# A hybrid decoder step: the sample group's HGRN update moved from the projection into the attention's filler work, and the page table read by one load

## The chip, the cores and the metric

One core of one Trainium2 chip. The metric is the device time of one execution in microseconds (us). A kernel's time is the median of several executions; the profile describes one execution.

## The reference, cut to what matters

One layer for two groups of tokens with the same weights: a prompt of 1024 tokens and a sample group of 8 sequences with one new token each and 1024 tokens of past. The layer is a projection (1024 to 3864 columns), a sparse attention with three branches (compressed, selected and window blocks; the sample group's past lies in paged caches), an HGRN2 recurrence with 4 heads of 128 x 128 state, an output projection and a gated embedding term.

The part that the change moves is the sample group's recurrence step. With one token per sequence it is, for every sequence b and head h,

```python
S_new = exp(log f)[..., None] * S + k[..., None] * v[None, :]
o = q @ S_new
```

where `S` (`state_hgrn`, 8 sequences x 4 heads x 128 x 128 fp32, 2 MB) is read, `S_new` is an output, and `o` is normalised and goes into the output projection. The page table (8 sequences x 8 pages, int32) gives for each sequence the rows of the caches: with 16 rows of a page on 16 partitions, partition p of column b needs `16 * page_table[b, p // 16] + p % 16`.

## The kernel before, in words

All matmuls work on fp32 numbers taken apart into a high and a low part: `split` (L50, L51) writes `hi` by a copy and `lo` by a subtraction, and `mm` (L42) is called with the combinations, so that most matmuls and casts carry the lines L42, L50 and L51. `load_w` (L222) loads weights in eight 128-row pieces (`w_raw`, L233, 3 buffers) and makes `w_hi` on ACT (L238) and `w_lo` on DVE (L239).

The program has these stages. Input tokens are loaded, normalised and transposed. The projection (`project`, L281) makes groups of columns: `tok` with tokens on partitions, `feat` with features on partitions. Between them stands the prompt group's recurrence: `hgrn_a` (L469) builds, per head, the masked products `AT` (with tiles `QK`, `PR`, `PQ` and predicated copies at L490, L513, L520 and L540), and `hgrn_b` (L566) makes states and outputs `O` (scaled at L608 on POOL, transposed at L612 on PE). The compressed keys follow, then the attention (`attention`, L618): 16 units of (128 queries, key group), cut into blocks. After every second block `attention` takes one step from the generator `side_work` (L640), which before holds the sample group's attention (`sample_attention`, L1000: gathers of cached rows into `sg`, stores of their second half to `VS`, window loads into `sg`, transposes, scores, softmax), and then the first steps of the last stage. The last stage is the output projection.

Each engine executes its instructions in a fixed order. That order is made when the kernel is built: a scheduler runs over all instructions with a cost model and priorities (the attention's blocks and the filler steps have their own), and it keeps the dependences and whatever `after` (L44) adds as an ordering without a semaphore. A DMA is issued from the queue of an engine; nearly all loads here are issued by SP, which also follows its order: an issue that has to wait for a buffer holds back the issues behind it.

The sample group's recurrence before is `hgrn_sample` (L422), a generator that `project` steps by hand, mostly around the last of the prompt's heads. For each head it loads the whole batch's state into a 128 x 1024 tile (L437, tag `S`) and the values, broadcast over the partitions, into another (`vb`, L439, tag `O`), from `v_d`, a copy of `vs` in DRAM. DVE multiplies `vb` by k (L441), POOL the state by f (L442), DVE adds (L443), SP stores the new state (L444), ACT and DVE split it into `S0h` and `S0l` (tag `F`), and PE makes 16 small matmuls per head with `qp`, a zeroed tile (L433) in which the 8 columns of q stand so that the results of all sequences and heads add up in one PSUM tile. Tags `S`, `O` and `F` are the ones that the prompt's recurrence uses: they share its buffers.

`page_index` (L645) reads the page table with 8 loads (L651) of 16 x 8 elements, each repeating a page number over 16 partitions, and makes `pidx` on DVE (L658). `project` calls it after the first recurrence heads; the scheduler may put its loads earlier.

Of the kernel before, what the change touches and what calls it, by code (L numbers as in the profile page):

```python
# [7 lines left out]
F32 = mybir.dt.float32  # L8
# [12 lines left out]
NB = 8  # L21
# [6 lines left out]
class Kernel:  # L28
# [195 lines left out]
    def load_w(self, src, *parts):  # L224

        nc = self.nc
        out = []
        width = sum(p[1] for p in parts)
        for k in range(8):
            raw = self.wpool.tile([128, 512], F32, name="w_raw", bufs=3)[:, :width]  # L230
            o = 0
            for c0, n in parts:
                dma = nc.sync.dma_start(raw[:, o:o + n], src[k * 128:(k + 1) * 128, c0:c0 + n])  # L233
# [13 lines left out]
        return out  # L247
# [32 lines left out]
    def project(self, ctx):  # L280
# [62 lines left out]
        go = lambda n: [next(smp, None) for _ in range(n)]  # L343
        for h in range(2, 4):
            st = self.hgrn_a(h, Q[h], K[h], F[h])
            go(2 if h == 3 else 0)
            self.hgrn_b(h, *st)
            go(1 if h == 3 else 0)

        def ev_z(dst, scale):  # L350
            def ev(f, ts, p):
# [38 lines left out]
        for _ in smp:  # L390
            pass
        self.aux_rows(hp)
        self.tok(C_KC, 256, ev_kv(0))
        self.tok(C_KS, 256, ev_kv(1))
# [24 lines left out]
                nc.sync.dma_start(self.V[:, br, :, h, :64], self.kv_d[1 + br].rearrange("(i p) c -> p i c", p=128)[:, :, 128 + 64 * h:192 + 64 * h])  # L419
        self.feat((C_ZB, 4, ev_z(self.zb_d, self.hgn)), ps=1)  # L420

    def hgrn_sample(self):  # L422

        nc, hp, a = self.nc, self.hp, self.a
        f, k, q = (self.sfkq[:, i] for i in range(3))
        v_d = self.dram.tile([NB, 512], F32, name="v_d")
        self.after(self.pidma, nc.sync.dma_start(v_d, self.vs))
        o = hp.tile([32, 128], F32, name="so", bufs=1)
        for h in range(4):
            yield  # L430
            po = self.ps_t.tile([128, 512], F32, name="pt")[:64, :128]
            qp = hp.tile([128, NB, 64], F32R, name="qp", bufs=1)
            nc.vector.tensor_scalar(qp.rearrange("p (a c) d -> p a (c d)", c=2), self.ones[:, None, :].to_broadcast([128, 4, 128]), 0.0, None, op0=OP.mult)  # L433
            qv = qp.rearrange("p b c -> p (b c)")
            self.split(qv[:, h * NB:h * NB + 456:65], qv[:, 32 + h * NB:32 + h * NB + 456:65], q[:, h], nc.vector, nc.vector)
            S = hp.tile([128, NB, 128], F32, name="S0", tag="S")
            nc.sync.dma_start(S, a["state_hgrn"][0, :, h].rearrange("b k v -> k b v"))  # L437
            vb = hp.tile([128, NB, 128], F32, name="vb", tag="O")
            nc.sync.dma_start(vb, bass.AP(tensor=v_d.tensor, offset=v_d.offset + h * 128, ap=[[0, 128], [512, NB], [1, 128]]))  # L439
            bc = lambda t: t[:, h, :, None].to_broadcast([128, NB, 128])  # L440
            nc.vector.tensor_tensor(vb, vb, bc(k), op=OP.mult)  # L441
            nc.gpsimd.tensor_tensor(S, S, bc(f), op=OP.mult)  # L442
            nc.vector.tensor_tensor(S, S, vb, op=OP.add)  # L443
            nc.sync.dma_start(a["hgrn_state_sample"][0, :, h].rearrange("b k v -> k b v"), S)  # L444
            hi = hp.tile([128, NB, 128], F32R, name="S0h", tag="F")
            lo = hp.tile([128, NB, 128], F32R, name="S0l", tag="F")
            self.split(hi, lo, S, nc.scalar, nc.vector)
            for b in range(NB):
                self.mm(po, qp[:, b], hi[:, b], b == 0, False)
                self.mm(po[:32], qp[:, b, :32], lo[:, b], False, b == NB - 1)  # L450
            if h:
# [4 lines left out]
        sq = hp.tile([32, 128], F32, name="ssq", bufs=1)  # L456
        ss = hp.tile([128, 1], F32, name="sr", bufs=1)[:32]
        nc.scalar.activation(sq, o, AF.Square, accum_out=ss)
        nc.vector.tensor_scalar(ss, ss, 1.0 / 128, EPS, op0=OP.mult, op1=OP.add)
        r = hp.tile([128, 1], F32, name="srs", bufs=1)[:32]  # L460
        self.rsqrt(hp, r, ss)
        nc.vector.tensor_scalar(o, o, r, None, op0=OP.mult)
        pt = self.ps_t.tile([128, 512], F32, name="pt")[:, :32]
        nc.tensor.transpose(pt, o, self.ident[:32, :32])
        oT = hp.tile([128, 32], F32, name="soT", bufs=1)
# [173 lines left out]

    def side_work(self):  # L640
        with ExitStack() as c:
            yield from self.sample_attention(c)
        yield from self.finish_setup(self.fctx)

    def page_index(self, pool):  # L645

        nc = self.nc
        pt = self.a["page_table"]
        raw = pool.tile([128, NB], I32, name="pt_raw", bufs=1)
        for i in range(8):  # L650
            dma = nc.sync.dma_start(raw[16 * i:16 * i + 16], bass.AP(tensor=pt.tensor, offset=pt.offset + i, ap=[[0, 16], [8, NB]]))  # L651
            if i == 0:
                self.pidma = dma
        lane = pool.tile([128, NB], I32, name="pt_lane", bufs=1)
        nc.gpsimd.iota(lane, pattern=[[0, NB]], base=0, channel_multiplier=1)
        nc.vector.tensor_scalar(lane, lane, 15, None, op0=OP.bitwise_and)
        self.pidx = self.cp.tile([128, NB], I32, name="pidx")
        nc.vector.scalar_tensor_tensor(self.pidx, raw, 16.0, lane, op0=OP.mult, op1=OP.add)  # L658
# [280 lines left out]
    def branches(self, qb, g, i):  # L939
# [455 lines left out]
```

## Time and profile before

| | |
|---|---|
| time, median of 3 runs | 1086.51 us (1083.82 to 1089.3) |
| time of the profiled execution | 1086.7 us |
| its span in the trace | 1085.0 us |
| mean granted TensorE clock | 0.991 of full speed |
| PE busy | 1047.7 us (97%) |
| DVE busy | 617.8 us (57%) |
| ACT busy | 388.4 us (36%) |
| POOL busy | 243.9 us (22%) |
| moved by DMA | 116.44 MB, mean 107 GB/s |

How to read the rows: times are in us from the start of the span. A row of the timeline has start, length, engine, line, operation, output tile <- input tiles, and in brackets how long the engine had been idle before it and what ended the wait. A row of the chain of waits has start, length and the work that the end of the program hung on at that time. A row of the windows has, for a stretch, the busy time of each engine with the number of instructions, the granted TensorE clock, the share of the 16 DMA engines and GB/s. Matmuls are pipelined: the length of one is longer than the distance to the next.

### The profile page before, as it was taken

The page shows a single profiled execution, that of the slowest core. Times are in us where ns is not written, and L with a number is a line of the kernel's source. Part 1 is how long each engine was busy: PE and PEld are TensorE (multiplying, and loading weights), DVE is VectorE, ACT ScalarE, POOL GpSimd, SP SyncE. Part 2 cuts the span into 40 slices and gives each one's busy share as a digit, 9 for nine tenths or more (in the row PEclk, how much of TensorE's full clock was granted, in tenths as well). Part 3 has the DMA queues.
Part 4 walks back from the last instruction along what each step waited for, and adds up shares of the span by engine and source line. Part 5 has one row for each costly group of instructions (what it writes and reads, how often), then busy time and mean ns, then how long its engine had stood idle before and what let it go on. Part 6 is the DMA issues. An engine that isn't in the chain of part 4 may idle for free.

```text
span 1085.0 us, 18918 instructions
## 1 busy us (share of the span) xinstructions
PE 1047.7 (97%) x7021; PEld 933.6 (86%) x7021; DVE 617.8 (57%) x1822; ACT 388.4 (36%) x786; POOL 243.9 (22%) x276
## 2 busy tenths in 40 slices
PE   4999999999899999999989999999999999999998
PEld 3898799999889899999968888888788888778876
DVE  6847565665494634543665656766665686471223
ACT  4622234313132335432234544553554232241112
POOL 0014232331041133002032211121323133131111
PEclk9999999999989999999989999999999999999999
DMA  6212023323464766403568611001831573121110
GB/s 195 79 29 69 11 72 100 117 89 119 131 176 142 214 210 211 148 1 107 129 215 266 154 29 51 20 21 53 227 106 40 161 209 90 41 97 49 49 35 30
DMA packets 118815, 116.44 MB, mean 107 GB/s; under 512 B 18710, under 2 KB 100974, under 8 KB 116420
## 3 DMA queue, kind: packets, MB, share of 16 engines
q1 hardware_dynamic: 97220, 79.46, 25.7%
q10 hardware_dynamic: 19200, 19.01, 5.1%
q0 software_dynamic: 2304, 16.78, 4.5%
q8 instruction: 55, 0.90, 0.4%
q14 instruction: 36, 0.29, 0.1%
HBM read 84.84 MB, written 29.31 MB: 105 GB/s over the span
## 4 chain that ended last, share of the span: by engine, by line
PE 82%; DMA 9%; DVE 4%; issue 2%; ACT 2%; POOL 1%; SPq 0%; ACTq 0%; DVEq 0%; POOLq 0%
PE pa L42 39%; PE pb L42 26%; PE ph L42 9%; PE pt L42 4%; DMA vb<-v_d 2%; DMA w_raw<-w_in 2%; PE ph L717 1%; PE pa L1125 1%; DMA fw_raw<-w_out 1%; DMA fw_raw<-ple_gate 1%; DMA x_in<-x_prompt 1%; DVE fw_lo L51 1%; PE ph L1319 1%; DMA gpre<-g_pre 0%; DMA f_oa<-oa_d 0%
## 5 line engine op out<-in xcount | busy, mean ns | idle before, releaser
L42 PEld LDWEIGHTS pb<-V,P 128*128 128x128 f32 x1056 | 141.8, 191 | 12.1 <-POOL P L960 1.2
L42 PE MATMUL pb<-V,P 128*128 128x128 f32 x1056 | 148.1, 276 | 0.4 <-DVE mx L909 0.4
L42 PE MATMUL pa<-xhi,w_hi 128*128 128x344 f32 x384 | 126.0, 330 | 2.6 <-ACT w_hi L238 1.1
L42 PE MATMUL pa<-xlo,w_hi 128*128 128x344 f32 x384 | 124.5, 326 | 0.0
L42 PE MATMUL pa<-xhi,w_lo 128*128 128x344 f32 x384 | 123.5, 327 | 0.0
L955 ACT ACTIVATE P<-ph 128x512 f32<-128x512 f32 (+4 forms) x148 | 85.6, 595 | 98.6 <-PE ph L42 69.3
L916 DVE CUSTOM_DVE_ANT_0 junk<-pa,mask 128x320 bf16<-128x320 f32 (+5 forms) x150 | 72.9, 497 | 27.8 <-PE pa L42 26.6
L42 PE MATMUL pa<-w_lo,xhi 128*128 128x256 f32 (+2 forms) x256 | 79.5, 314 | 0.0
L42 PE MATMUL pa<-w_hi,xlo 128*128 128x256 f32 (+2 forms) x256 | 79.2, 314 | 0.0
L42 PE MATMUL pa<-w_hi,xhi 128*128 128x256 f32 (+2 forms) x256 | 78.6, 316 | 0.0
L42 PEld LDWEIGHTS pa<-xhi,w_hi 128*128 128x128 f32 x384 | 73.5, 192 | 4.2 <-ACT w_hi L238 1.7
L238 ACT ACTIVATE w_hi<-w_raw,gpre 128x512 fp32r<-128x512 f32 (+2 forms) x80 | 47.5, 616 | 78.2 <-DMA w_raw<-w_in 43.0
L42 PEld LDWEIGHTS pa<-xlo,w_hi 128*128 128x128 f32 x384 | 73.5, 192 | 0.1
L42 PEld LDWEIGHTS pa<-xhi,w_lo 128*128 128x128 f32 x384 | 73.0, 191 | 0.2
L42 PE MATMUL ph<-QA,KA 128*128 128x512 f32 (+4 forms) x148 | 66.7, 453 | 3.8 <-ACT P L955 2.9
L42 PE MATMUL pa<-KB,QB 65*128 65x320 f32 (+6 forms) x195 | 63.4, 363 | 0.1
L239 DVE SCALAR_TENSOR_TENSOR w_lo<-w_raw,gpre,w_hi 128x512 fp32r<-128x512 f32 (+2 forms) x80 | 50.6, 653 | 21.4 <-ACT w_hi L238 20.7
L42 PE MATMUL pa<-fw_hi,yh 128*128 128x512 f32 (+1 forms) x160 | 61.9, 387 | 0.2 <-ACT fw_hi L50 0.2
L42 PE MATMUL pa<-fw_lo,yh 128*128 128x512 f32 (+1 forms) x160 | 61.6, 385 | 0.0
L42 PE MATMUL pa<-fw_hi,yl 128*128 128x512 f32 (+1 forms) x160 | 61.6, 385 | 0.0
L42 PE MATMUL ph<-QB,KB 68*128 68x512 f32 (+4 forms) x148 | 58.5, 406 | 0.0
L559 POOL TENSOR_TENSOR K<-K,E 128x512 f32<-128x512 f32 x24 | 36.4, 1517 | 94.2 <-PE pb L42 57.2
(457 smaller groups left out, 2411.9 us busy)
## 6 DMA issues: line engine op xcount, KB each, us to landing
w_raw<-w_in SPq DMA_DIRECT2D x32, 256.0 KB
w_raw<-w_in SPq DMA_DIRECT2D x48, 128.0 KB
VS<-sg SPq DMA_DIRECT2D x8, 512.0 KB
sg<-cache_win_kv SPq DMA_DIRECT2D x16, 256.0 KB
fw_raw<-w_out SPq DMA_DIRECT2D x16, 256.0 KB
fw_raw<-ple_gate SPq DMA_DIRECT2D x16, 256.0 KB
f_x<-x_prompt SPq DMA_DIRECT2D x8, 512.0 KB
win_kv_sample<-cache_win_kv SPq DMA_DIRECT2D x8, 511.0 KB
```

What stands on the lines that cost most here:

```text
L42: return self.nc.tensor.matmul(out, lhsT, rhs, start=start, stop=stop, skip_group_check=True)
L51: lo_eng.tensor_tensor(lo, src, hi.bitcast(F32), op=OP.subtract)
L238: nc.scalar.activation(hi, raw, AF.Copy, scale=g)
L239: nc.vector.scalar_tensor_tensor(lo, raw, g, hi.bitcast(F32), op0=OP.mult, op1=OP.subtract)
L559: nc.gpsimd.tensor_tensor(Kv[:, :, 0], Kv[:, :, 0], Ev[:, :, 1:2].to_broadcast([128, nb, m]), op=OP.mult)
L717: nc.tensor.transpose(pt[:, i * 128:(i + 1) * 128], src[b0 + j // 2, kv][:, j % 2, 2 * jp:2 * jp + 2].rearrange("p j d -> p (j d)"), self. ...
L916: nc.vector.tensor_tensor_reduce(junk, pm, mk, 1.0, -1e30, op0=OP.add, op1=OP.max, accum_out=o)
L955: nc.scalar.activation(P, ps, AF.Exp, scale=0.125)
L1125: nc.tensor.transpose(pt[:, j * 128:(j + 1) * 128], rows(j), self.ident)
L1319: nc.tensor.transpose(pt[:, c], h[:, k * 128:(k + 1) * 128], self.ident[:n, :n])
```

## The change

1. The sample group's recurrence becomes 8 pieces of (head, 4 sequences), with tiles of 128 x 512 in a pool of their own (`hS` and `hvb` with two buffers each; `hSh`, `hSl` and `qp` with one), and with PSUM tiles of the attention's pool. Loads are two pieces ahead: load(0) and load(1), then update(i), product(i), load(i + 2). It leaves the projection; `side_work` takes one step of it beside each step of the sample group's attention from the seventh on. `gated` orders its loads, updates and products after the attention's last QA matmul emitted so far (`anchor`), for the scheduler only.
2. The copy `v_d` of the values is stored from `project`, as before after the page table's load.
3. The page table is read by one 8 x 8 load, ordered after the last weight load issued so far (`lastw`). A selector matrix made on POOL (`sel`, a `z_s` tile) and a 128 x 8 matmul repeat the numbers over the partitions, with two casts on DVE.

```diff
-                dma = nc.sync.dma_start(raw[:, o:o + n], src[...])
+                dma = self.lastw = nc.sync.dma_start(raw[:, o:o + n], src[...])
...
-        smp = self.hgrn_sample()
-        next(smp)
+        self.v_d = self.dram.tile([NB, 512], F32, name="v_d")
+        self.after(nc.sync.dma_start(self.v_d, self.vs), self.pidma)
...
-    def hgrn_sample(self):
+    def hgrn_sample(self, ctx):
+        hp = self.pool(ctx, "hsamp", side="right")
+        pieces = [(h, b0) for h in range(4) for b0 in (0, 4)]
+        gated = lambda x: self.after(x, self.anchor)
+        def load(i):
+            S = hp.tile([128, 4, 128], F32, name="hS", bufs=2)
+            gated(nc.sync.dma_start(S, a["state_hgrn"][0, b0:b0 + 4, h].rearrange("b k v -> k b v")))
+            vb = hp.tile([128, 4, 128], F32, name="hvb", bufs=2)
+            gated(nc.sync.dma_start(vb, ...))
+        def update(i):
+            gated(nc.vector.tensor_tensor(vb, vb, bc(k), op=OP.mult))
+            gated(nc.gpsimd.tensor_tensor(S, S, bc(f), op=OP.mult))
+            nc.vector.tensor_tensor(S, S, vb, op=OP.add)
+            gated(nc.sync.dma_start(a["hgrn_state_sample"][0, b0:b0 + 4, h]..., S))
+            self.split(hi, lo, S, nc.scalar, nc.vector)
+        load(0)
+        yield
+        load(1)
+        yield
+        for i in range(8):
+            update(i)
+            yield
+            product(i)
+            yield
+            if i < 6:
+                load(i + 2)
+                yield
...
     def side_work(self):
         with ExitStack() as c:
-            yield from self.sample_attention(c)
+            state = self.hgrn_sample(c)
+            for j, _ in enumerate(self.sample_attention(c)):
+                if j >= 6:
+                    next(state, None)
+                yield
+            for _ in state:
+                yield
...
-        raw = pool.tile([128, NB], I32, name="pt_raw", bufs=1)
-        for i in range(8):
-            dma = nc.sync.dma_start(raw[16 * i:16 * i + 16], bass.AP(..., ap=[[0, 16], [8, NB]]))
+        raw = pool.tile([8, NB], I32, name="pt_raw", bufs=1)
+        self.pidma = nc.sync.dma_start(raw, bass.AP(..., ap=[[1, 8], [8, NB]]))
+        self.after(self.pidma, self.lastw)
...
-                    self.mm(ps, KA[br, g][:, ks], QA, True, False)
+                    self.anchor = self.mm(ps, KA[br, g][:, ks], QA, True, False)
```

Line numbers in the rows of order that follow are each kernel's own. The first place is DVE in the projection, where the last of the prompt's heads makes `AT` (L490, L513, L520 and L540 before are L512, L535, L542 and L562 in the change; `z_s` is a projected group on its way to DRAM). Before:

```order
397 L51 TENSOR_TENSOR PRl<-PR,PRh 128x512
398 L369 COPY z_s<-pa 128x256
399 L441 TENSOR_TENSOR vb<-vb,sfkq 128x1024
400 L520 COPY_PREDICATED AT<-lm_496,ph 128x512
401 L51 TENSOR_TENSOR PQl<-PQ,PQh 128x1024
402 L490 COPY_PREDICATED AT<-lm_495,pt 128x512
403 L369 COPY z_s<-pa 128x256 x2
404 L441 TENSOR_TENSOR vb<-vb,sfkq 128x1024
405 L513 COPY_PREDICATED AT<-lm_498,ph 128x256x2
406 L513 COPY_PREDICATED AT<-lm_497,ph 128x256x2
```

The same place in the changed kernel:

```order
385 L51 TENSOR_TENSOR PRl<-PR,PRh 128x512
386 L365 COPY z_s<-pa 128x256
387 L542 COPY_PREDICATED AT<-lm_496,ph 128x512
388 L51 TENSOR_TENSOR PQl<-PQ,PQh 128x1024
389 L512 COPY_PREDICATED AT<-lm_495,pt 128x512
390 L365 COPY z_s<-pa 128x256
391 L535 COPY_PREDICATED AT<-lm_498,ph 128x256x2
392 L535 COPY_PREDICATED AT<-lm_497,ph 128x256x2
```

The two `vb` rows are gone, and one `z_s` row stands later; the rest keeps its order.

The second place is the start of SP's queue. Before:

```order
3 L190 DMA x_in<-x_sample 8x1024
4 L233 DMA w_raw<-w_in 128x256 x6
5 L651 DMA pt_raw<-page_table 16x8x1 x7
6 L233 DMA w_raw<-w_in 128x256 x10
7 L233 DMA w_raw<-w_in 128x512 x8
8 L244 DMA win_kv_sample<-cache_win_kv 16x8176 x2
```

In the changed kernel:

```order
3 L190 DMA x_in<-x_sample 8x1024
4 L233 DMA w_raw<-w_in 128x256 x16
5 L233 DMA w_raw<-w_in 128x512 x8
6 L244 DMA win_kv_sample<-cache_win_kv 16x8176 x2
7 L678 DMA pt_raw<-page_table 8x8x1
8 L233 DMA w_raw<-w_in 128x256 x8
```

Seven of the eight small loads stood between the first weight loads; the one load now stands behind two groups of weights.

The third place is the attention, where the new pieces begin. SP in the changed kernel (L429 and L431 load state and values, L446 stores a state, L1191 is `VS`, L921 the next unit's queries):

```order
91 L1076 DMA gate<-g_d 64x3
92 L1191 DMA VS<-sg 128x8x128 x4
93 L429 DMA hS<-state_hgrn 128x4x128 x2
94 L431 DMA hvb<-v_d 128x4x128 x2
95 L921 DMA QB_5298<-qh_d 64x4x128
96 L1191 DMA VS<-sg 128x8x128
97 L921 DMA QA<-qh_d 64x4x128
98 L921 DMA QA<-ql_d 64x4x128
99 L446 DMA hgrn_state_sample<-hS 128x4x128
```

And DVE in the changed kernel, where piece 0 is updated (L1178 before is L1141, L953 before is L916):

```order
695 L1178 TENSOR_TENSOR s_6025<-s_6025,bi 64x1024
696 L443 TENSOR_TENSOR hvb<-hvb,sfkq 128x512
697 L445 TENSOR_TENSOR hS<-hS,hvb 128x512
698 L51 TENSOR_TENSOR KT_6166<-pa,KT_6165 128x512
699 L51 TENSOR_TENSOR hSl<-hS,hSh 128x512
700 L51 TENSOR_TENSOR KT_6211<-pa,KT_6210 128x512
701 L953 ISA junk,mx<-pa,mask 128x320
```

The four loads stand between the fourth and the fifth `VS` store, and the update between the scores' bias and the split of a gathered key.

## Rows read from the trace of the kernel before

**Rows 1.** The page, busy time of each engine.

```profile
PE 1047.7 (97%) x7021; PEld 933.6 (86%) x7021; DVE 617.8 (57%) x1822; ACT 388.4 (36%) x786; POOL 243.9 (22%) x276
```

**Rows 2.** Waits of PE, whole span: line, releaser, us in total, times, longest.

```profile
PE ph L42 <- DVE AT L513: 3.6, 1, 3.6
PE ph L42 <- DVE AT L520: 2.9, 1, 2.9
...
PE pt L612 <- POOL O L608: 2.6, 1, 2.6
```

**Rows 3.** Windows: stretch, length, busy PE, PEld, DVE, ACT, POOL, clock, DMA.

```profile
275.00:300.00 25.00, 19.15 (x138) 18.07 (x137) 10.37 (x16) 2.72 (x8) 0.56 (x1) 1.00 0.47 131
350.00:375.00 25.00, 22.43 (x146) 22.12 (x145) 13.68 (x27) 9.29 (x22) 5.38 (x6) 0.93 0.68 206
...
300.00:308.00 8.00, 7.33 (x37) 7.12 (x38) 6.76 (x8) 2.03 (x4) 5.50 (x3) 0.58 0.53 161
364.00:370.00 6.00, 6.00 (x31) 5.99 (x32) 1.41 (x4) 2.64 (x5) 0.00 (x0) 0.72 0.66 222
```

**Rows 4.** The chain of waits, parts of 14 to 366: start, us, what.

```profile
20.64 7.24 DMA w_raw<-w_in
...
277.76 4.18 DMA kv_d<-z_s
...
282.81 5.47 DMA vb<-v_d
...
291.91 6.10 DMA vb<-v_d
...
351.77 7.82 DMA vb<-v_d
...
361.05 2.86 POOL O L608
```

**Rows 5.** Timeline of ACT and of PE, 27 to 33.

```profile
27.96 0.72 ACT L238 ACTIVATE w_hi<-w_raw,gpre 128x512 fp32r<-128x512 f32 x1 [6.01 <-DMA w_raw<-w_in]
...
28.73 0.42 PE L42 MATMUL pa<-xhi,w_hi 128*128 128x344 f32 x1 [0.91 <-ACT w_hi L238]
...
32.98 0.42 PE L42 MATMUL pa<-xhi,w_hi 128*128 128x344 f32 x1 [0.20 <-ACT w_hi L238]
```

**Rows 6.** The tile S: ns of one (min/median/max), first and last start.

```profile
L442 POOL TENSOR_TENSOR S<-S,sfkq x4: 1898/1900/2495, 300.1 to 354.4; 128x1024 f32<-128x1024 f32 x4
L443 DVE TENSOR_TENSOR S<-S,vb x4: 1203/1218/2155, 302.1 to 360.9; 128x1024 f32<-128x1024 f32 x4
```

**Rows 7.** The tile qp.

```profile
L433 DVE TENSOR_SCALAR qp<-ones x4: 404/411/995, 3.1 to 375.9; 128x512 fp32r<-128x512 f32 x4
...
L51 DVE TENSOR_TENSOR qp<-sfkq,qp x4: 155/161/170, 78.3 to 379.3; 128x8 fp32r<-128x8 f32 x4
```

**Rows 8.** The tile sg; the last row is from issue to landing, of all its DMAs.

```profile
L50 ACT CAST KT<-sg x8: 612/620/622, 681.4 to 737.5; 128x512 fp32r<-128x512 f32 x8
L51 DVE TENSOR_TENSOR KT<-sg,KT x8: 679/689/710, 682.2 to 738.4; 128x512 fp32r<-128x512 f32 x8
...
DMA to landing us min/median/max: 5.6/6.8/9.6
```

**Rows 9.** Windows in the attention.

```profile
570.00:580.00 10.00, 10.00 (x74) 8.61 (x73) 7.73 (x31) 4.45 (x10) 3.17 (x4) 1.00 0.89 298
610.00:620.00 10.00, 10.00 (x65) 8.63 (x66) 9.15 (x30) 5.05 (x10) 3.84 (x5) 1.00 0.23 60
570.00:690.00 120.00, 119.62 (x842) 105.50 (x841) 73.44 (x271) 58.07 (x107) 26.28 (x36) 1.00 0.41 115
```

**Rows 10.** Timeline of SP and of DVE in the attention.

```profile
571.84 0.59 SPq L1154 DMA_DIRECT2D VS<-sg  x1
...
578.64 1.21 DVE L1141 TENSOR_TENSOR s<-s,bi 64x1024 f32<-64x1024 f32 x1
...
601.87 0.69 DVE L51 TENSOR_TENSOR KT<-pa,KT 128x512 fp32r<-128x512 f32 x1 [4.27 <-ACT KT L50]
```

More of the change, by code (lines that the diff above doesn't have):

```diff
@@ L342, in project @@
         self.feat((C_QB + 256, 2, ev_q(2)))
-        go = lambda n: [next(smp, None) for _ in range(n)]
         for h in range(2, 4):
[L345 to L348, printed above, removed]
+            self.hgrn_b(h, *self.hgrn_a(h, Q[h], K[h], F[h]))
         def ev_z(dst, scale):
@@ L420, in project @@
         self.feat((C_ZB, 4, ev_z(self.zb_d, self.hgn)), ps=1)
-    def hgrn_sample(self):
-        nc, hp, a = self.nc, self.hp, self.a
+    def hgrn_sample(self, ctx):
+        nc, a = self.nc, self.a
         f, k, q = (self.sfkq[:, i] for i in range(3))
[L426 to L433, printed above, removed]
-            qv = qp.rearrange("p b c -> p (b c)")
[L435 to L442, printed above, removed]
@@ new lines, in hgrn_sample @@
+        hp = self.pool(ctx, "hsamp", side="right")
+        o = hp.tile([32, 128], F32, name="so")
+        pieces = [(h, b0) for h in range(4) for b0 in (0, 4)]
+        held = {}
+        gated = lambda x: self.after(x, self.anchor)
+        def load(i):
+            h, b0 = pieces[i]
+            S = hp.tile([128, 4, 128], F32, name="hS", bufs=2)
+            gated(nc.sync.dma_start(S, a["state_hgrn"][0, b0:b0 + 4, h].rearrange("b k v -> k b v")))
+            vb = hp.tile([128, 4, 128], F32, name="hvb", bufs=2)
+            gated(nc.sync.dma_start(vb, bass.AP(tensor=self.v_d.tensor, offset=self.v_d.offset + b0 * 512 + h * 128, ap=[[0, 128], [512, 4], [1, 128]])))
+            held[i] = S, vb
@@ new lines, in update @@
+        def update(i):
+            h, b0 = pieces[i]
+            S, vb = held[i]
+            qp = hp.tile([128, 4, 64], F32R, name="qp")
+            gated(nc.vector.tensor_scalar(qp.rearrange("p (a c) d -> p a (c d)", c=2), self.ones[:, None, :].to_broadcast([128, 2, 128]), 0.0, None, op0=OP.mult))
+            qv = qp.rearrange("p b c -> p (b c)")
+            c0 = h * NB + b0
+            self.split(qv[:, c0:c0 + 196:65], qv[:, 32 + c0:32 + c0 + 196:65], q[:, h, b0:b0 + 4], nc.vector, nc.vector)
+            bc = lambda t: t[:, h, b0:b0 + 4, None].to_broadcast([128, 4, 128])
+            gated(nc.vector.tensor_tensor(vb, vb, bc(k), op=OP.mult))
+            gated(nc.gpsimd.tensor_tensor(S, S, bc(f), op=OP.mult))
@@ L443, in hgrn_sample @@
             nc.vector.tensor_tensor(S, S, vb, op=OP.add)
-            nc.sync.dma_start(a["hgrn_state_sample"][0, :, h].rearrange("b k v -> k b v"), S)
-            hi = hp.tile([128, NB, 128], F32R, name="S0h", tag="F")
-            lo = hp.tile([128, NB, 128], F32R, name="S0l", tag="F")
+            gated(nc.sync.dma_start(a["hgrn_state_sample"][0, b0:b0 + 4, h].rearrange("b k v -> k b v"), S))
+            hi = hp.tile([128, 4, 128], F32R, name="hSh")
+            lo = hp.tile([128, 4, 128], F32R, name="hSl")
@@ L447, in hgrn_sample, with product @@
             self.split(hi, lo, S, nc.scalar, nc.vector)
[L448 to L451, printed above, removed]
+            held[i] = qp, hi, lo
+        def product(i):
+            qp, hi, lo = held[i]
+            po = self.ps_a.tile([128, 512], F32, name="pa")[:64, :128]
+            for b in range(4):
+                m = self.mm(po, qp[:, b], hi[:, b], b == 0, False)
+                if b == 0:
+                    gated(m)
+                self.mm(po[:32], qp[:, b, :32], lo[:, b], False, b == 3)
+            if i:
@@ L648, in page_index @@
         pt = self.a["page_table"]
-        raw = pool.tile([128, NB], I32, name="pt_raw", bufs=1)
-        for i in range(8):
-            dma = nc.sync.dma_start(raw[16 * i:16 * i + 16], bass.AP(tensor=pt.tensor, offset=pt.offset + i, ap=[[0, 16], [8, NB]]))
-            if i == 0:
-                self.pidma = dma
+        raw = pool.tile([8, NB], I32, name="pt_raw", bufs=1)
+        self.pidma = nc.sync.dma_start(raw, bass.AP(tensor=pt.tensor, offset=pt.offset, ap=[[1, 8], [8, NB]]))
+        self.after(self.pidma, self.lastw)
+        num = pool.tile([8, NB], F32, name="pt_num", bufs=1)
+        nc.vector.tensor_copy(num, raw)
+        sel = self.zpool.tile([128, 688], F32, name="z_s", bufs=2)[:8, :128]
+        nc.gpsimd.memset(sel, 1.0)
+        nc.gpsimd.affine_select(sel, sel, pattern=[[1, 128]], compare_op=OP.is_ge, fill=0.0, base=0, channel_multiplier=-16)
+        nc.gpsimd.affine_select(sel, sel, pattern=[[-1, 128]], compare_op=OP.is_ge, fill=0.0, base=15, channel_multiplier=16)
         lane = pool.tile([128, NB], I32, name="pt_lane", bufs=1)
@@ L656, in page_index @@
         nc.vector.tensor_scalar(lane, lane, 15, None, op0=OP.bitwise_and)
+        lf = pool.tile([128, NB], F32, name="pt_lf", bufs=1)
+        nc.vector.tensor_copy(lf, lane)
+        p = self.ps_t.tile([128, 512], F32, name="pt")[:, :NB]
+        self.mm(p, sel, num, True, True)
         self.pidx = self.cp.tile([128, NB], I32, name="pidx")
-        nc.vector.scalar_tensor_tensor(self.pidx, raw, 16.0, lane, op0=OP.mult, op1=OP.add)
+        nc.vector.scalar_tensor_tensor(self.pidx, p, 16.0, lf, op0=OP.mult, op1=OP.add)
     def gather(self, out, cache, b):
```

14 lines of the change are left out of this document (6 added, 8 removed).

## The prediction

> **What bounds the kernel now.** I read the page first: PE is busy for 1047.7 of 1085.0 us [rows 1], so 37.3 us of PE idleness, and time in which PE runs at a lower clock, are all that a change of order can win; no other engine is over 57%. The list of PE's waits says where: besides the start of the program, where PE waits for the first input, three waits of one occurrence each stand out, 3.6 and 2.9 us for predicated copies into `AT` and 2.6 us for `O` [rows 2]. All three fall into the two stretches where the sample group's recurrence runs. The windows show them as holes: PE is busy 19.15 of 25 us in one and 22.43 in the other [rows 3], and behind each hole the granted clock is lower, 0.58 of full over 300 to 308 and 0.72 over 364 to 370 [rows 3], after PE had been idle; a mean of that kind is 2.4 GHz mixed with 1.2.
>
> The chain of waits then names what stands behind the copies: the load of `vb` from `v_d` on DRAM, 5.47 and 6.10 us in the first place and 7.82 in the second [rows 4]. DVE takes the multiply of `vb` in its fixed order, so it stands still until the load has landed, and the copies into `AT`, which PE needs, are queued behind it. In the second place it is the scaling of `O` on POOL (2.86 us in the chain [rows 4]) that came late, since DVE, which makes its factor, stood at `vb` as well. These are waits for data that could have been loaded long before, not a lack of an engine.
>
> **What the change removes.** In the first place DVE's order loses both `vb` rows and keeps the rest. The gain there is 3.60 + 2.92 = 6.5 us of idleness [rows 2] and the clock: 8 us at 0.58 are 8 x 0.42 = 3.4 us of full-speed work lost [rows 3], which come back if the holes that preceded them are gone. That makes 9.9 us. Bounds: 0 if another wait is right behind (a rival, below), 9.9 if none.
>
> In the second place: 2.57 us (2.6 in the list [rows 2]), and 6 us x 0.28 = 1.7 us of clock [rows 3]: 4.3 us; bounds 0 and 4.3.
>
> At the start, seven loads of single elements no longer stand ahead of the third `w_raw` group in SP's queue. A weight load that was issued behind them takes 7.24 us in the chain [rows 4]; ACT waits 6.01 us for it, but PE, fed by earlier weights, waits only 0.91 and later 0.20 us [rows 5]. The gain is what PE waited, 1.1 us; bounds 0 and 1.1. The new page-table path (a memset, two selects, two casts, a 128 x 8 matmul) costs POOL, DVE and PE well under 1 us each beside a projection in which PE has a queue of work; its consumer, the first gather, comes some 400 us later. I take nothing for it. Should that cover be missing, its longest chain of small operations, at 0.16 to 0.41 us each [rows 7], is some 2 us.
>
> Sum of the gains: 9.9 + 4.3 + 1.1 = 15.3 us.
>
> **What the change adds in the attention.** The 64 small matmuls are the same in number and shape, and PE is the bound in both places: no difference. DVE gets, per piece, three 128 x 512 operations at 0.69 us [rows 8] and five small ones between 0.16 and 0.41 us [rows 7]: 2.9 to 4.1 us, over 8 pieces 23 to 33. I take 25, since the small ones have only 4 columns or 32 partitions but for one. ACT gets 8 x 0.62 = 5 us [rows 8], POOL 8 multiplies of half the width of one that took 1.90 [rows 6], so 0.95 to 1.9 us each. Over 570 to 690, where the pieces run, DVE is now busy 73.44 of 120 us (61%) [rows 9]; with 25 more it is 82%. It stays below PE's 119.62. In the busiest 10 us it would be 9.15 [rows 9] + 25/12 = 11.2: one microsecond late there, which the next stretch takes up. So engine time alone is hidden; its cover is that PE's queue reaches several units ahead, and the trace has a measure of it: at 601.87 DVE had waited 4.27 us [rows 10] while PE was idle for only 0.38 us in the whole 120 us [rows 9].
>
> What is not sure to be hidden is new waiting for loads. Piece 0's four loads are issued directly behind the fourth `VS` store at 571.84 [rows 10], so at about 572.5 to 574.5 with 0.6 us each, while DMA is 89% busy [rows 9]. DVE comes to its multiply behind the bias of `s`, at 578.64 + 1.21 = 579.85 [rows 10]. Loads of that size take 5.6 to 9.6, mostly 6.8 us [rows 8]: the values of piece 0 land between 579 and 583, and the state needs POOL's multiply yet. So DVE stands for 0 to 4 us, say 3. From piece 2 on a state load cannot go before the store of the piece two earlier; reading the order of SP against POOL with the times that neighbouring rows had before, the state loads stand 4 to 9 us ahead of their use, against 6.8 to land. I estimate 1 to 2 us each for four of these. Together DVE or POOL waits some 9 us, none of it longer than the 4.27 that passed without a trace. At no cover at all, 9 us would cost 9 x 1.5 = 13.5 us, with the clock in the proportion of the present holes ((6.5 + 2.6 + 3.4 + 1.7) / (6.5 + 2.6) = 1.5); at full cover 0. I take 6, a little under the middle, because of the row at 601.87.
>
> The sum: 1086.7 - 15.3 + 6 = 1077.4, for the profiled execution, which is 0.2 us above the median of 1086.51. **Forecast 1077.5 us.** Its own range is 1071 to 1081.
>
> Against splitting the transfers speaks the Trainium skill, page "DMA: Bandwidth & Descriptors", section on rules for kernel authors, which says to coalesce many small transfers into one large one, and gives about 2.0 us of fixed time to each DMA; 24 instead of 12 would by it cost an estimated 24 us, if none of it were hidden, and the time would be about 1095. What the trace shows is that the large ones, 512 KB, took 5.5 to 7.8 us [rows 4] and the mix of 256 and 512 KB 6.8 [rows 8]: a half-size load is hardly shorter, and its time counts only where an engine stands waiting for it.
>
> **Rivals.**
>
> *The waits only move.* The 9 us of new waiting meet PE uncovered, since DVE at 82% has little slack to catch up and the exponentials' tiles run out: 13.5 us lost, 1086.7 - 15.3 + 13.5 = 1084.9. For it: DMA is 89% busy where the pieces begin [rows 9], and `hSh` stands in ACT's queue ahead of the exponentials. Against: the pieces are spread over 120 us, and PE there hardly waits now. Chance 0.18.
>
> *The holes stay half open.* With `vb` gone, DVE's next rows in the first place still depend on others, such as `z_s`, which has two buffers and whose store to `kv_d` takes 4.18 us in the chain [rows 4], just ahead of the first hole. If one of the two holes comes back with its clock, half of 9.9 is lost: 1077.4 + 5 = 1082.4. Against: such a store held DVE before the first hole without a PE wait in the list. Chance 0.10.
>
> *Late loads in every piece, slower than before.* The place is POOL's and DVE's queue at each piece's first multiply. A state load stands about 6 us ahead of use; with landing time L and 1.5 us for POOL, DVE waits L - 4.5, of which 4.3 are covered. At L = 11 us each of eight pieces would leave PE idle for 2.2 us, 17.6 in all, with the clock 26: 1086.7 - 15.3 + 26 = 1097. It decides from the point where 20.7 us (15.3 and 5.4) are lost, so 20.7 / 1.5 / 8 = 1.7 us a piece, or L = 10.5 us. For it: the stretch from 570 has DMA at 89% and 298 GB/s [rows 9], and the longest landing among these was 9.6 [rows 8]. Against: from 610 on DMA is 23% busy [rows 9], so that at most three pieces are loaded in the crowd. It is the rule above turned into a mechanism. Chance 0.10.
>
> *The change does all it says and hides everything*: 1086.7 - 15.3 = 1071.4. This is the lower end of the forecast, part of its 0.62.
>
> **How the numbers follow.** A measurement of this kernel can tell about 0.5% from no change, 5.4 us: below 1081.1 is faster, above 1091.9 slower. The forecast (0 to 9 us lost) has 0.62 and is faster; moved waits and half-open holes, 0.18 + 0.10, come out at 1082 to 1085, the same; late loads, 0.10, slower. The range for 8 in 10 runs from 1071, all gains and no loss, to 1087, which takes in both middle cases and leaves the slow one and some of the edges out.
>
> **What would show it.** Right: no wait of PE for `AT` or for `O` of more than 1 us around 285 to 305 and 360, a granted clock of 1.00 there, and the attention starting some 15 us earlier; ACT's wait for the third weight group shorter by 3 us or more; in the attention, multiplies of `hvb` and `hS` with waits of 0 to 4 us for DMA, and PE idle 2 to 6 us more in total over the pieces than now. Wrong: PE waits at the same place in the projection for another releaser (holes half open); PE busy under 95% in the stretch of the pieces with a clock under 0.95 (waits moved); landing times over 10 us for the state loads, at each piece (slower).

## The result, and the profile after

The changed kernel took 1096.78 us (median of 6 runs, 1094.07 to 1098.01) against 1087.16 for the kernel before in the same comparison: a ratio of 1.0075 (95% interval 1.0051 to 1.01), slower by 8 us where 9 faster was forecast, and outside the range. The profiled execution has a span of 1095.2 us. The medians of the kernel before went from 1087.2 to 1089.5 between the comparisons that follow, so runs are compared by their ratios; one hundredth is 10.9 us.

On the page of the changed kernel PE is idle for 1095.2 - 1058.6 = 36.6 us, no more than before [rows 1]:

```profile
PE 1058.6 (97%) x7023; PEld 938.9 (86%) x7023; DVE 620.9 (57%) x1856; ACT 389.8 (36%) x790; POOL 241.4 (22%) x283
```

What has grown most in this pair of profiles is the time at the lower clock: the mean granted clock fell from 0.991 to 0.984, (1 - 0.984) x 1095.2 = 17.5 us of full-speed work lost instead of 9.8. That is 7.7 of the 10.2 us by which the span grew. The holes in the projection are gone, as the windows of the changed kernel show beside [rows 3], and others have come in the attention:

```profile
275.00:300.00 25.00, 25.00 (x203) 24.11 (x205) 15.57 (x29) 5.76 (x13) 2.84 (x3) 1.00 0.26 82
...
300.00:308.00 8.00, 8.00 (x138) 7.71 (x138) 5.60 (x9) 3.57 (x7) 2.15 (x2) 1.00 0.62 175
600.00:640.00 40.00, 35.27 (x195) 29.41 (x194) 26.52 (x90) 14.62 (x26) 9.24 (x11) 0.79 0.25 71
```

From 600 to 640 PE is idle for 4.7 us, and at a clock of 0.79 another 40 x 0.21 = 8.4 us of full-speed work are lost. The list of PE's waits no longer has `AT` and `O` [rows 2]; in their place:

```profile
PE pa L42 <- DVE mx L953: 3.1, 1, 3.1
PE ph L754 <- DVE cr L747: 2.3, 1, 2.3
```

The tile `QA` gives the attention's length. Its matmuls run, in the kernel before and then in the changed one (last columns: first and last start, shapes):

```profile
L42 PE MATMUL ph<-QA,KA x148: 391/474/795, 547.3 to 845.6; 128*128 128x512 f32 x132, 128*47 128x512 f32 x2, 128*55 128x512 f32 x2, 128*63 128x512 f32 x2
```

```profile
L42 PE MATMUL ph<-QA,KA x148: 390/453/795, 528.2 to 855.6; 128*128 128x512 f32 x132, 128*47 128x512 f32 x2, 128*55 128x512 f32 x2, 128*63 128x512 f32 x2
```

The attention starts 19.1 us earlier and lasts 327.4 instead of 298.3 us: 29.1 longer. 3.8 us in both numbers are the 64 small matmuls, 0.06 us apart, that moved. So 15.3 us were won ahead of it and 25.3 lost in it.

The largest hole, in the timeline of SP, POOL, DVE and PE of the changed kernel:

```profile
592.44 3.79 SPq L1154 DMA_DIRECT2D sg<-cache_win_kv  x4
596.34 0.71 SPq L429 DMA_DIRECT2D hS<-state_hgrn  x1
...
602.85 1.04 POOL L444 TENSOR_TENSOR hS<-hS,sfkq 128x512 f32<-128x512 f32 x1 [7.23 <-DMA hS<-state_hgrn]
...
603.92 1.10 DVE L445 TENSOR_TENSOR hS<-hS,hvb 128x512 f32<-128x512 f32 x1 [5.31 <-POOL hS L444]
...
605.68 0.37 PE L42 MATMUL pa<-hSh,qp 128*64 128x128 f32 x1 [3.14 <-DVE mx L953]
```

A state load stands behind window loads on SP, POOL waits for it, DVE for POOL, and PE's next instruction is the small matmul of a product: its PSUM tile `pa` is still held by a maximum that DVE, behind its wait, has not taken. It is the only place in the attention where PE waits for `pa` ahead of a product. This looks like a load that is late. The experiments say otherwise.

### The profile page after: what moved, and what is told of

It is laid out like the page before. It is cut to its first block, busy times and chain, and to the rows that moved or that the text cites. A ratio compares the mean times of both kernels' runs of the same rounds, so it can differ in the third digit from the quotient of the medians.

```text
span 1095.2 us, 18956 instructions
## 1 busy us (share of the span) xinstructions
PE 1058.6 (97%) x7023; PEld 938.9 (86%) x7023; DVE 620.9 (57%) x1856; ACT 389.8 (36%) x790; POOL 241.4 (22%) x283
## 5 line engine op out<-in xcount | busy, mean ns | idle before, releaser
L42 PEld LDWEIGHTS pb<-V,P 128*128 128x128 f32 x1056 | 146.2, 198 | 13.4 <-issue 1.5
L42 PE MATMUL pb<-V,P 128*128 128x128 f32 x1056 | 154.3, 284 | 0.8 <-DVE pb L1016 0.4
L953 DVE CUSTOM_DVE_ANT_0 junk<-pa,mask 128x320 bf16<-128x320 f32 (+5 forms) x150 | 72.8, 494 | 16.8 <-PE pa L42 15.0
L42 PE MATMUL pa<-KB,QB 65*128 65x320 f32 (+6 forms) x195 | 66.7, 374 | 1.3 <-ACT QB L972 0.9
L239 DVE SCALAR_TENSOR_TENSOR w_lo<-w_raw,gpre,w_hi 128x512 fp32r<-128x512 f32 (+2 forms) x80 | 54.9, 706 | 18.8 <-ACT w_hi L238 16.9
L581 POOL TENSOR_TENSOR K<-K,E 128x512 f32<-128x512 f32 x24 | 34.2, 1424 | 115.1 <-PE pb L42 53.7
L42 PE MATMUL ph<-QB,KB 68*128 68x512 f32 (+3 forms) x148 | 59.1, 413 | 0.0
```

What stands on the lines that cost most here:

```text
L42: return self.nc.tensor.matmul(out, lhsT, rhs, start=start, stop=stop, skip_group_check=True)
L581: nc.gpsimd.tensor_tensor(Kv[:, :, 0], Kv[:, :, 0], Ev[:, :, 1:2].to_broadcast([128, nb, m]), op=OP.mult)
L953: nc.vector.tensor_tensor_reduce(junk, pm, mk, 1.0, -1e30, op0=OP.add, op1=OP.max, accum_out=o)
```

## The experiments

Every run was compared with the kernel before on the same chip. The sum of them, as ratios and in us over the changed kernel without the step (e2); an interval is 2 to 4 us to each side (5 for e10), so that differences under some 4 to 5 us are not told apart. e2, e3, e5, e6 and e13 leave out parts of the layer's work, as said at each:

| run | what it is | ratio (95% interval) | over e2 |
|---|---|---|---|
| - | the change | 1.0075 (1.0051 to 1.01) | 20.7 |
| e1 | before, with the new page table | 0.9949 (0.9927 to 0.9971) | 7.0 |
| e2 | the change without the step | 0.9885 (0.9853 to 0.9917) | 0 |
| e3 | no loads for pieces 2 to 7 | 1.0069 (1.0037 to 1.0101) | 20.0 |
| e4 | from the 21st step on | 1.0081 (1.0054 to 1.0108) | 21.3 |
| e5 | without DVE's updates | 0.9928 (0.9903 to 0.9952) | 4.7 |
| e6 | without the products | 0.995 (0.9922 to 0.9977) | 7.1 |
| e7 | two hSh and hSl | 1.0058 (1.0035 to 1.0082) | 18.8 |
| e8 | beside every 2nd step | 0.9955 (0.993 to 0.998) | 7.6 |
| e9 | e1, step later in projection | 1.0078 (1.0049 to 1.0107) | 21.0 |
| e10 | e7, product after next update | 1.0124 (1.0075 to 1.0173) | 26.0 |
| e11 | two operations on POOL | 0.9971 (0.9948 to 0.9995) | 9.3 |
| e12 | e8 and e11 | 0.996 (0.9939 to 0.9981) | 8.2 |
| e13 | DVE's instructions alone | 0.9901 (0.9867 to 0.9935) | 1.7 |
| e14 | beside every 3rd step | 0.996 (0.9936 to 0.9984) | 8.2 |
| e15 | every 2nd step, from the first | 0.9935 (0.991 to 0.9961) | 5.4 |
| e16 | product emptied by ACT and POOL | 1.009 (1.0059 to 1.0121) | 22.3 |
| e17 | product's tile from ph | 0.9913 (0.9879 to 0.9947) | 3.0 |
| e18 | e15 and e17 | 0.9895 (0.9868 to 0.9921) | 1.1 |

**e1, e2: the parts of the change.** e1 is the kernel before with the diff's `page_index`, `lastw` and order of `v_d`; e2 keeps of `hgrn_sample` only its pool, one `yield` and:

```diff
+        oT = hp.tile([128, 32], F32, name="soT")
+        nc.scalar.copy(oT, self.ident[:, :32])
+        nc.scalar.dma_start(self.oT_d[:, :, T:].rearrange("h v b -> v h b"), ...)
```

> The kernel before with the change's page table alone (one 8 x 8 load behind two groups of weights, matmul with a selector); the sample group's recurrence stays in the projection as before. Theory: the changed kernel reaches its second group of projection matmuls 3.9 us earlier (73.3 against 77.2 us) because of this part, so 1083.3 us against 1087.2, with PE's waits for AT and O (3.6, 2.9 and 2.6 us) still there. Rival: the 3.9 us come from the scheduler's other order at the start and not from the small loads; then about 1086.

> The changed kernel without the sample group's recurrence: its loads, updates, products and state stores are left out, a constant is stored in place of its result. Theory (all of the loss is made by the pieces in the attention, 25 us and 3.8 us of small matmuls): 1096.8 - 29 = 1068 us, PE idle under 2 us from the attention's start to its unit at 664 us. Rival (the attention that starts 19 us earlier meets its gathers and loads worse, whatever the pieces do): 1080 or more, with PE holes in the attention that stay.

e1 measured 1083.52 us: the theory held, and PE's waits for `AT` and `O` are still in its list. e2 measured 1075.12, between the theory and its rival. Its attention starts as early as the change's, yet it gives back some 6 us with no piece in it:

```profile
L42 PE MATMUL ph<-QA,KA x148: 387/474/795, 527.9 to 832.4; 128*128 128x512 f32 x132, 128*47 128x512 f32 x2, 128*55 128x512 f32 x2, 128*63 128x512 f32 x2
```

It takes 304.5 us against 298.3. And e1 to e2 is 0.0064, 7 us, of which 3.8 are matmuls: hiding the step's waits completely could in the end win some 3 us by these two runs, not the 14 that stood in the holes.

**e3, e4: the loads.** e3, where pieces 2 to 7 work on the tiles of the first two, and e4, which begins later:

```diff
-                load(i + 2)
+                held[i + 2] = tiles[i + 2] = tiles[i]
```

```diff
-                if j >= 6:
+                if j >= 20:
```

> The changed kernel with all of the pieces' arithmetic and stores, but pieces 2 to 7 work on the tiles of the first two instead of loading their own: only the 12 later loads are left out. Theory (late loads: POOL's multiply waits for the state behind SP's window loads, DVE stands 5 us twice, PE runs out and its clock falls): 1072 to 1077, DVE's waits for the state below 1 us, no half clock from 600 to 640. Rival (it is the added work on DVE, ACT and POOL, or its places in their queues): 1090 or more.

> The changed kernel with the pieces beginning at the 21st step of the sample group's attention instead of the 7th, which puts their loads behind the window loads that fill the DMA queues from 550 to 600 us; all work is kept. Theory (late loads): in the quiet stretch a state load lands in about 2.8 us, DVE waits little, 1072 to 1080. Rival (the added work costs PE wherever it stands in the attention): 1090 or more.

1095.55 and 1097.52 us, both the rival's: late loads are not the cause. With 12 of the 16 loads gone the time is the change's within the intervals, though DVE's waits for POOL at `hS`, 12.4 us in the change, have left the list. e3's windows show the same picture, only elsewhere (PE's busy time is the second number, the clock the number after POOL's):

```profile
640.00:660.00 20.00, 17.03 (x99) 12.72 (x99) 14.38 (x48) 7.77 (x14) 4.50 (x6) 0.91 0.33 93
660.00:670.00 10.00, 10.00 (x32) 7.50 (x30) 4.44 (x19) 2.81 (x7) 0.00 (x0) 0.50 0.00 0
```

What PE waits for there, in e3's timeline of PE, is again `pa` and a maximum, in a row of small holes with no DMA among the releasers:

```profile
647.48 0.41 PE L42 MATMUL pa<-KB,QB 65*128 65x320 f32 x1 [0.28 <-DVE mx L954]
...
649.60 0.41 PE L42 MATMUL pa<-KB,QB 65*128 65x320 f32 x1 [0.47 <-DVE mx L954]
```

**e5, e6, e7, e8: the work, the product, the buffers, the density.** e5, where `qp` is also filled only once and the products take `hi` for `lo`; e6, where the sums are dropped too; e7, where the tile `ssq` also moves into a buffer of `hvb`; and e8:

```diff
-            gated(nc.vector.tensor_tensor(vb, vb, bc(k), op=OP.mult))
...
-            nc.vector.tensor_tensor(S, S, vb, op=OP.add)
...
-            self.split(hi, lo, S, nc.scalar, nc.vector)
+            lo = hi
+            nc.scalar.copy(hi, S)
```

```diff
-                m = self.mm(po, qp[:, b], hi[:, b], b == 0, False)
...
-                self.mm(po[:32], qp[:, b, :32], lo[:, b], False, b == 3)
```

```diff
-            hi = hp.tile([128, 4, 128], F32R, name="hSh")
-            lo = hp.tile([128, 4, 128], F32R, name="hSl")
+            hi = hp.tile([128, 4, 128], F32R, name="hSh", bufs=2)
+            lo = hp.tile([128, 4, 128], F32R, name="hSl", bufs=2)
```

```diff
-                if j >= 6:
+                if j >= 6 and j % 2 == 0:
```

> The changed kernel without DVE's part of the updates: the multiply by k, the add, the low part of the split and the filling of qp for pieces 1 to 7 are left out (2.7 us of DVE a piece, some 21 us); all loads, stores, POOL's multiply, ACT's copy, the products and the two small adds stay, so the result is not the recurrence's. Theory 1 (DVE, already loaded in bursts, is late for PE): 1080 to 1084, PE's waits on DVE gone, clock near 0.99. Theory 2 (the product in PE's queue with its single buffers and shared PSUM tiles): 1092 or more.

> The changed kernel without the products: the 64 small matmuls and the adds of their results are left out, the output rows of the recurrence are a constant; loads, the whole update and the stores stay. The matmuls themselves are 3.8 us. Theory 1 (DVE's update work): 1088 to 1093, so 4 to 8 us less than the changed kernel. Theory 2 (the product's place in PE's queue, its PSUM tile and the single hSh and hSl that make ACT and DVE wait for it): 1078 or less.

> The changed kernel with two buffers instead of one for hSh and hSl, so that ACT's copy and DVE's subtraction need not wait for the product of the piece before (ACT waits 5.5 us in five such places now). Theory 1 (DVE's work): within 3 us of the changed kernel's 1096.8. Theory 2 (the coupling by single buffers): 1080 to 1088.

> The changed kernel with a step of the recurrence only beside every second step of the sample group's attention, the rest after it: the same work over about twice the time. Theory 1 (bursts on DVE): less density, 1080 to 1088. Theory 2 (each product and update makes its own hole wherever it stands): 1093 to 1099, as many half-clock stretches, only farther apart.

1082.29, 1083.40, 1095.13 and 1082.86 us: theory 1 for e5, e7 and e8, and neither theory for e6, which lies between them. Over e2, the step without its products costs 7.1 us (e6), and without DVE's part of the updates 4.7, of which 3.8 are the matmuls (e5). Neither half costs much without the other; together, in dense steps, they cost 20.7. Second buffers for `hSh` and `hSl` do not help, half the density does. Since removing either side helps alike, "DVE's time" was not yet told from a tie between the two.

**e9: the step later in the projection**, e1 with:

```diff
-            go(2 if h == 3 else 0)
-            go(1 if h == 3 else 0)
...
         self.tok(C_KC, 256, ev_kv(0))
+        go(1)
         self.tok(C_KS, 256, ev_kv(1))
+        go(2)
         self.tok(C_KW, 280, ev_kv(2))
+        for _ in smp:
+            pass
```

> The kernel before with the new page table, and with the sample group's recurrence still in the projection in its old form (4 heads, 128 x 1024 tiles, shared buffers), but its steps are emitted after the last of the prompt's recurrence heads, between the three last groups of the projection. Theory (the holes at AT came from DVE standing at vb ahead of the prompt's copies): no wait of PE for AT, 3.5 + 1.8 us of idleness and some 3.4 us of clock less than the run with the page table alone (1083.5): 1074 to 1077. Rival (DVE's wait for vb of 5 to 8 us only moves to a later place where PE waits for it): 1082 or more.

1097.10 us: the rival, and worse. `AT` has left the list of PE's waits, but the chain of e9 still hangs on `vb`, three times. The two longest of these loads are issued behind the store of the state before them (SP at 334.58 and 345.58 us), so behind the update before:

```profile
335.58 7.40 DMA vb<-v_d
...
346.02 7.21 DMA vb<-v_d
```

**e10, e11, e12: three ways to loosen the dense steps.** e10, on top of e7, with the filling of `qp` moved into `product` and `product(7)` behind the loop; e11; and e12, which is e8 with e11's edit:

```diff
             update(i)
             yield
-            product(i)
-            yield
+            if i:
+                product(i - 1)
+                yield
```

```diff
-            gated(nc.vector.tensor_tensor(vb, vb, bc(k), op=OP.mult))
+            gated(nc.gpsimd.tensor_tensor(vb, vb, bc(k), op=OP.mult))
...
-            nc.vector.tensor_tensor(S, S, vb, op=OP.add)
+            nc.gpsimd.tensor_tensor(S, S, vb, op=OP.add)
```

> The changed kernel with two hSh and hSl, and each product emitted after the next piece's update instead of behind its own, qp filled with the product: same work in the same steps, but PE and DVE need not answer each other within a piece. Theory 1 (density of work on DVE in its bursts): 1092 to 1097. Theory 2 (DVE, ACT and PE wait for each other within a piece): 1080 to 1086.

> The changed kernel with the multiply by k and the add on POOL instead of DVE: 1.4 us a piece, 11 us, leave DVE, and what DVE waited for the state (5.0 and 5.3 us) is waited on POOL; steps as dense as in the change. Theory 1 (DVE's work and waits): 1085 to 1090. Rival (any work in a dense row of steps costs, since POOL also makes the masks of P): 1094 or more.

> Both remedies together: a step beside every second step of the sample group's attention, and the multiply by k and the add on POOL. Theory 1: they add in part, 1078 to 1081. Rival (what the spreading leaves, 1082.9, is not DVE's): 1082 or more.

1104.17, 1086.15 and 1084.54 us. e11 gave 11 us, as theory 1 had it; e12 says that what is left after spreading is not DVE's multiply and add. e10 was a clear miss of both theories: slower. Its cause was not looked for; PE waited 4.6 us for `pa` behind maxima, in three places.

**e13: DVE's time by itself**, with e14 and e15 on the density (`j >= 6 and j % 3 == 0`, and `j % 2 == 0`). e13:

```diff
-            gated(nc.sync.dma_start(S, ...))
+            gated(nc.gpsimd.memset(S, 0.5))
...
-            gated(nc.gpsimd.tensor_tensor(S, S, bc(f), op=OP.mult))
-            self.split(hi, lo, S, nc.scalar, nc.vector)
+            nc.vector.tensor_tensor(lo, S, vb, op=OP.subtract)
...
-                nc.vector.tensor_tensor(o, o, po[:32], op=OP.add)
+                nc.vector.tensor_tensor(o, o, vb[:32, 0], op=OP.add)
```

> The changed kernel with only DVE's instructions of the step, the same shapes at the same steps (25 us in all), on tiles filled once with a constant: no loads, no stores, no POOL, no ACT and no PE work of the pieces, and nothing in them that waits for another engine; the recurrence's results are left out. The floor without the step is 1075.1. Theory 1 (DVE's time alone, in dense steps): 1083 to 1090, so more than half of the 18 us that the pieces cost beyond their 3.8 us of matmuls. Theory 2 (DVE's time is hidden, what costs is the chain through loads, POOL, ACT, DVE and PE in their fixed orders): under 1079.

> As the run with a step beside every second step of the sample group's attention, but every third. Theory 1 (density): 1079 to 1083. Rival (beyond every second step nothing is left to win, and the rest falls into the stretch from 750 on, where PE now waits too): 1083 to 1090.

> A step beside every second step of the sample group's attention, from its first step instead of its seventh, so that fewer steps are left for the stretch from 750 on. Theory 1: 1078 to 1083. Rival (the first pieces meet the attention's start, where PE is at half clock and its queue short): 1084 or more.

1078.21 us for e13: 1.7 us over e2. Theory 1 falls: DVE's work in dense steps (22 us more busy than in e2, 615.0 against 593.2) is hidden when nothing in it is tied to another engine. e14 (1084.36) and e15 (1082.23) cannot be told from e8: spreading the steps further than beside every second one brings nothing more.

**e16, e17, e18: the tie.** What the product shares with the prompt's blocks is its PSUM tile. e16, and e17, which changes one line:

```diff
-            nc.vector.tensor_tensor(o, o, po[:32], op=OP.add)
...
+            nc.scalar.copy(pc[:, 0], po[:32])
+            nc.scalar.copy(pc[:, 1], po[32:])
...
+            nc.gpsimd.tensor_tensor(o, o, pc[:, 0], op=OP.add)
```

```diff
-            po = self.ps_a.tile([128, 512], F32, name="pa")[:64, :128]
+            po = self.ps_h.tile([128, 512], F32, name="ph")[:64, :128]
```

> The changed kernel, steps as dense as in the change, but the product's sum leaves PSUM by two copies on ACT and is added up on POOL, so that the product's tile pa (three buffers, shared with the maxima and the transposes) is given back without DVE, and DVE has no instruction that waits for a product's matmuls but qp's filling. Theory (the product ties PE to DVE through pa: PE stands at the product until DVE has freed a buffer, and DVE stands at the sums until PE is through): 1083 to 1088. Rival (the product costs by its place in PE's queue, whoever empties its tile): 1093 or more.

> The changed kernel with the product's PSUM tile taken from ph (two buffers, of the scores that ACT makes into P) instead of pa (three, of the maxima that DVE reads); all else as in the change. Theory (pa as the tie between PE and DVE): 1085 to 1092, with PE waits for P on ACT a little longer instead. Rival (any shared tile ties): 1096 or more.

> The product's tile from ph, and a step beside every second step of the sample group's attention from its first on. Theory (both remedies remove the same waits: with the tile in ph the dense steps already run at 100 of 100 us of PE and full clock from 600 to 700): 1077 to 1081, no better than the tile alone at 1079.4. Rival (they add): 1075 or less.

e16 measured 1098.20 us: emptying the tile by ACT instead of DVE does not help, so the part of its theory that has PE wait for DVE's sums falls. e17 measured 1079.43, more than the theory asked: 3.0 us over e2, about the 3.8 us of matmuls that it contains. All loads, all of DVE's updates and the dense steps are still there. PE in e17's window against the change's, in that order:

```profile
600.00:700.00 100.00, 100.00 (x788) 90.03 (x787) 78.60 (x285) 51.17 (x94) 23.81 (x31) 1.00 0.21 59
```

```profile
600.00:700.00 100.00, 92.80 (x637) 78.63 (x635) 74.72 (x261) 44.30 (x82) 22.50 (x28) 0.91 0.23 61
```

DVE is even busier in e17, 78.6 of 100 us, and in this window PE has no hole and the full clock. Not in all of the attention: from 731 to 751 us e17 runs at half clock too, and PE was not idle before it. It had just made 16 matmuls of 8 columns each:

```profile
728.54 1.95 PE L42 MATMUL pt<-two,o 16*128 16x8 f32 x16
...
731.00:751.00 20.00, 20.00 (x75) 16.85 (x74) 10.40 (x44) 5.19 (x9) 3.79 (x6) 0.50 0.29 86
```

Over its profiled execution e17 has a mean clock of 0.984, the same as the change; over six executions each, the means of 0.988 and 0.984 make some 4 of the 17 us between them. So the gain is not mainly one of clock: in the profiles PE is idle for 1078.9 - 1050.3 = 28.6 instead of 36.6 us, and busy for 8.3 us less.

The scheduler's order changes with the tile. In the change the first product starts 24 us behind ACT's first copy into `hSh`, and PE's order has transposes and maxima that also take `pa` before it; in e17 it starts 3 us behind. The first two rows are the change's, the others e17's (behind the three durations: first and last start):

```profile
L42 PE MATMUL pa<-hSh,qp x32: 221/224/368, 588.9 to 682.4; 128*64 128x128 f32 x32
L50 ACT CAST hSh<-hS x8: 612/619/623, 564.8 to 674.3; 128x512 fp32r<-128x512 f32 x8
```

```profile
L42 PE MATMUL ph<-hSh,qp x32: 218/223/304, 566.0 to 640.3; 128*64 128x128 f32 x32
L50 ACT CAST hSh<-hS x8: 610/618/619, 562.7 to 636.6; 128x512 fp32r<-128x512 f32 x8
```

What is shown is therefore the tile together with the order that it allows; the two were not taken apart, and a run with the change's order and `ph`, or e17's order and `pa`, is missing. The late product alone is not the cost either: in e8 it starts 33 us behind the first copy, and e8 is 13 us faster than the change. e18 measured 1077.48 us, as its theory said within what can be told: the remedies overlap. It is the fastest version that does all of the layer's work, ratio 0.9895 (0.9868 to 0.9921) to the kernel before.

## Why the prediction was wrong

*The gain ahead of the attention* was put at 9.9 + 4.3 + 1.1 = 15.3 us and came out at 15.3 in the trace, but by errors that cancel, which is luck. The start gave 3.9, not 1.1: the second group's first matmul with `w_lo` is at 73.5 instead of 77.4 us,

```profile
L42 PE MATMUL pa<-w_lo,xhi x256: 276/287/435, 77.4 to 306.6; 128*128 128x256 f32 x64, 128*128 128x512 f32 x32, 128*128 128x280 f32 x32
```

```profile
L42 PE MATMUL pa<-w_lo,xhi x256: 276/288/403, 73.5 to 293.4; 128*128 128x256 f32 x64, 128*128 128x512 f32 x32, 128*128 128x280 f32 x32
```

since PE not only lost the 1.1 us of waits [rows 5] but, for a part of the rest, also left its slow stretch earlier: in the changed kernel's timeline one 344-column matmul follows another after 0.16 us from 24.89 on, in the kernel before from 27.04 on, and 0.29 before that. The last of these matmuls comes 13.2 us earlier, so 9.3 more for the first place, where 9.9 stood. The second place, with what follows it up to the attention, gave the rest, 19.1 - 13.2 - 3.8 = 2.1 instead of 4.3; a new wait of 2.3 us for `cr`, listed above, is a part of it. The mechanism was right: with the `vb` rows out of DVE's order those holes are gone, and in e1, which keeps them, they stay.

*That such a gain reaches the end* was assumed and is wrong in part: without any piece (e2) the attention still gave back 6 us.

*The added waits for loads* were put at 9 us. POOL waited 13.6 us for states in five places and DVE 12.4 for POOL in four. The two overlap, since POOL's wait is DVE's. That is more than 9, and e3 shows that it hardly counts: without most of those loads the time is the same.

*DVE's time* was said to be hidden, and e13 bears it out at 1.7 us.

*The step that failed* is the first sentence of the part on the attention: "The 64 small matmuls are the same in number and shape, and PE is the bound in both places: no difference." The instructions are the same, the tile is not. Before, the products went into `pt`; now they take one of three `pa` buffers, which the prompt's maxima and the sample group's transposes use all the time. With it the dense pieces cost 20.7 us, with `ph` 3.0. In the sum the attention's term stood at 6 us and came out at 25.3. Whether PE pays by waiting for the tile or by the order that the scheduler makes for it stays open; the direct waits for `pa` ahead of a product are 3.1 us. The second size that failed is the price of a hole: 1.5 us per us of idleness, from the holes in the projection. In the attention 4.7 us of idleness went with 8.4 us of clock (600 to 640), which makes 2.8, and in e17 the clock fell to half with no idleness before it. So no fixed price of a hole follows from these traces.

*The rivals.* "Late loads in every piece" named 1097, and 1096.78 came: the right number by the wrong mechanism. Its place was POOL's and DVE's first multiply and its condition landings over 10.5 us; they were at most 9.4 (issued at 573.64, in use at 583.00), and about 3 us once the windows were loaded. No run bears out a cost for each DMA either: twelve fewer changed nothing here (e3). The Trainium skill, page "DMA: Bandwidth & Descriptors", section "Rules for kernel authors", states the coalescing rule for many small transfers and names 64 KB; the 2.0 us stand in another section of that page, fitted to DMAs issued from gpsimd. The loads here are of 256 KB and issued by SP, so the estimate of 1095 stretched both. "The holes stay half open" did not come: no wait for `AT` or `O` is left. "The waits only move" was the nearest: its sign, PE busy under 95% with a clock under 0.95 in the stretch of the pieces, came (113.72 of 120 us and 0.93 from 570 to 690), but it named the exponentials, not `pa`.

## What to carry to other kernels

When work is moved next to other work, list what it shares there besides engine time, PSUM and SBUF tags first: here the choice of tag, with the order that follows from it, made 20.7 or 3.0 us of the same 3.8 us of matmuls. The number of buffers does not tell which tag is cheap: `pa` has three, `ph` two. If PE waits for a buffer that a third party's consumer holds, try another pool before touching loads or density. And test the wait that the trace shows by removing it: here the most visible one, a late load, was worth nothing that could be measured.

## What had not been expected of the hardware

Little or no idleness can go with a large loss of clock. In e3 PE, after 3.0 us of short waits in 20 us, ran at 0.50 of its clock, 1.2 GHz, for the whole of the next 10 us while being busy all the time; in e17 it did so for 20 us behind 16 matmuls of 8 columns, with no wait before (rows above). A state load of 256 KB took 2.8 us in a quiet stretch (issued at 623.55, used at 626.36); one issued at 573.64 and one at 596.34 were used 9.4 and 6.5 us later, and the DMA engines' busy share is 1.04 from 550 to 600.
